# A matmul–GELU–matmul kernel: one store of the first result block moves from SyncE's DMA queue to GpSimd's

## The chip, the cores and the metric

The kernel runs on one core of one Trainium2 chip. The metric is the device time of one execution in microseconds (us), shown as the median of nine runs. A core has five engines with instruction streams of their own: TensorE (PE; its weight loads are a row of their own, PEld), VectorE (DVE), ScalarE (ACT), GpSimd (POOL) and SyncE (SP). They meet only through semaphores. SP computes nothing; here it issues DMAs and waits. A lower-case q after an engine's name (SPq) means its sequencer.

## The reference

```python
a: (1024, 1024), b: (1024, 2048), c: (2048, 1024), all float32, normal draws
h = np.matmul(a, b)
h = 0.5 * h * (1 + np.tanh(np.sqrt(2 / np.pi) * (h + 0.044715 * h ** 3)))
return np.matmul(h, c).astype(np.float32)
```

The result is 1024 x 1024 float32, 4 MiB, in rows of 128 (eight row tiles) by two halves of 512 columns.

## The kernel before

**Work.** `a` is loaded, cast to bf16 and transposed on PE; `b` and `c` are loaded and cast. The first product with GELU gives `h` transposed in bf16 (`hT`). Both products run in part or whole through the class `Seven`: a 2 x 2 block product in seven block products in place of eight, with sums and differences of blocks (`s1` to `s4` of the left factor, `t1` to `t4` of the right one) made on DVE in pieces of 128 x 1024. The object `two` is the second matrix product; `seven(two, done2, between2)` (L406) runs it. Its steps, in the order in which the program writes them: the block product P1, P2, P5, P6, P7, then the third and fourth ones. `between2` (L390) issues the DVE work between the steps: after P2 `two.s2(4)` and `two.s3(4)`, after P5 `two.t3(4)` and `two.s4(...)`, after P7 `two.t4`. All of it is one order written out by hand (`tc.manual_schedule()`), each engine runs its list in that order.

**Result tiles.** A finished 128 x 512 piece of the result is a tile `ot`, made by DVE: `plus` (L289, add of PSUM and a saved partial sum, at L291), or the copy at L386 in `done2`. These tiles turn in four buffers (tag "o"), so the fifth one must wait until the first one's store has landed. The first three come from P2 (blocks (0,0), j = 0, 1, 2: rows 0 to 383 of the left half), the fourth and fifth are the j = 0 and j = 1 tiles of P7. The last row tile of block (0,0) (j = 3) is done at the very end, in two pieces of 128 x 256 (L340 to L343).

**Stores.** `done2(i, l, j, p)` (L383) calls `store` (L380), which issues one DMA on the queue of the engine `eng`, or on SP's where none is given:

```python
def store(mt, q0, w, ot, eng=None):
    (eng or nc.sync).dma_start(out=out[ts(mt, 128), ds(q0, w)], in_=ot)
```

SP issues 8 loads (L68, L71) at the start and then all 17 stores: 15 of 256 KB (L381 from `done2`) and 2 of 128 KB (L381 from L343). POOL issues 20 loads (L93, L96, L99, L102), the last at 36.4 us, and nothing after them but the end of the program.

**Semaphores of the DMAs.** The framework gives every DMA of SP's queue one of eight semaphores in turn, DMAHW0 to DMAHW7, here called lanes, and every DMA of POOL's queue one of eight others, DMASW0 to DMASW7. A DMA adds 16 to its lane when all of it has landed. Before a DMA takes a lane again, its engine waits for the one that had it, eight DMAs earlier on the same queue. At the end of the program (the profile puts this at L432) SP waits for the final count of every lane, one instruction after the other, in this order:

```
1  DMASW7, DMASW6            6  DMAHW4, DMASW1
2  DMAHW0, DMASW5            7  DMAHW5, DMASW0
3  DMAHW1, DMASW4            8  DMAHW6, DVE
4  DMAHW2, DMASW3            9  DMAHW7, ACT
5  DMAHW3, DMASW2            then two drains, and a barrier of all engines
```

In the barrier each engine reports with a drain, POOL gathers the reports and releases all. SP's queue has 8 + 17 = 25 DMAs, numbers 0 to 24. The last store is number 24 and has lane DMAHW0, the one before it lane DMAHW7.

Of the kernel before, what the change touches and what calls it, by code (L numbers as in the profile page):

```python
# [19 lines left out]
def kernel(ctx, tc, a, b, c, out):  # L20
    nc = tc.nc
# [3 lines left out]
    H = 512  # L25
# [17 lines left out]
    def bank(i, shape=(128, H), dt=F32, name="ps"):  # L43
        return pp.tile(list(shape), dt, name=name, tag=f"bank{i}", padded_shape=None)

    def pieces(tag, bufs, shape, dt, name):
        return small.tile(shape, dt, name=name, tag=tag, bufs=bufs)
# [219 lines left out]
    p = bank(7)  # L267
# [4 lines left out]
    for n in range(8):  # L272
        h, t = divmod(n, 4)
        p = bank(n)
# [105 lines left out]
    def store(mt, q0, w, ot, eng=None):  # L380
        (eng or nc.sync).dma_start(out=out[ts(mt, 128), ds(q0, w)], in_=ot)  # L381

    def done2(i, l, j, p):  # L383
        if (i, l) == (1, 0):
            ot = pieces("o", 4, [128, H], F32, "ot")
            nc.vector.tensor_copy(ot, p)  # L386
            p = ot
        store(4 * i + j, l * H, H, p)

    def between2(n):  # L390
        if n == "P1":
# [11 lines left out]
        elif n == "P73":  # L403
            two.t4(two.t[1], 4)

    seven(two, done2, between2)  # L406


# [28 lines left out]
```

## Time and profile before

| | |
|---|---|
| median of 9 runs | 120.52 us (120.37 to 120.74) |
| the profiled execution | 120.40 us, of which the span of the profile is 118.6 us |
| granted TensorE clock | 0.996 |
| PE busy | 111.9 us (94% of the span) |
| DVE busy | 88.5 us (75%) |
| ACT busy | 52.7 us (44%) |
| POOL busy | 14.6 us (12%) |
| DMA, SP's queue (q1) | 5648 packets, 8.39 MB |
| DMA, POOL's queue (q0) | 5952 packets, 8.39 MB |
| HBM | 20.97 MB read, 4.19 MB written |

The span runs from the first instruction to the last; 1.8 us of the execution's time lie outside it. PE is busy nearly throughout, but that says nothing of the last microseconds: there the work is over and the program waits for its last store and closes. Times below are counted from the start of the span.

### The profile page before, as it was taken

Reading aid. Unit: us, or ns where it says so; the run is one execution under the profiler, and the core shown is the slowest. Engines: PE = TensorE matmul, PEld = TensorE weight load, DVE = VectorE, ACT = ScalarE, POOL = GpSimd, SP = SyncE. Lnnn points to the kernel's source line nnn. Section 1 sums busy time; section 2 is a strip of 40 time slices with the busy share of each in tenths; the row PEclk is TensorE's granted clock in tenths of the full one; section 3 lists DMA queues with packets and bytes.
Section 4 is the critical chain, followed back from the end, with each engine's and each line's share of the span. In section 5 each row is a group of like instructions: output and inputs, shape, how many; then the busy total and the mean of one; then the engine's idle time right before and its main releaser. Section 6 shows DMA issues by size and latency. Waiting matters only on the chain.

```text
span 118.6 us, 1473 instructions
## 1 busy us (share of the span) xinstructions
PE 111.9 (94%) x558; PEld 72.9 (61%) x558; DVE 88.5 (75%) x93; ACT 52.7 (44%) x86; POOL 14.6 (12%) x27
## 2 busy tenths in 40 slices
PE   6887999999999999999999999999999999999970
PEld 2544445654444446888886444588888888888850
DVE  0243689489058899796879999999999986944760
ACT  5046491006657789856589348700033982000000
POOL 2003976363222000000000000000000000000000
PEclk9999999999999999999999999999999999999998
DMA  3999999999999999994000000070000002024992
GB/s 91 293 371 369 338 202 211 198 205 205 208 210 210 211 210 211 211 211 88 3 3 0 6 0 0 0 265 0 0 0 0 6 4 84 0 93 176 361 351 81
DMA packets 11606, 16.86 MB, mean 142 GB/s; under 512 B 720, under 2 KB 6096, under 8 KB 11600
## 3 DMA queue, kind: packets, MB, share of 16 engines
q0 software_dynamic: 5952, 8.39, 39.8%
q1 hardware_dynamic: 5648, 8.39, 20.2%
q8 instruction: 4, 0.07, 0.2%
q14 instruction: 2, 0.02, 0.0%
HBM read 20.97 MB, written 4.19 MB: 212 GB/s over the span
## 4 chain that ended last, share of the span: by engine, by line
PE 86%; DMA 7%; SPq 2%; DVE 1%; issue 0%; DVEq 0%
PE ps L241 63%; PE ps L112 20%; DMA sta<-in_a_dram 7%; PE pt L187 2%; SPq L68 1%; SPq L71 1%; DVE ab L108 1%; PE pt L135 1%; DVE ot L342 0%; DVEq L108 0%
## 5 line engine op out<-in xcount | busy, mean ns | idle before, releaser
L112 PE MATMUL ps<-aT,b 128*128 128x512 bf16 x128 | 29.2, 379 | 1.4 <-DVE aT L136 0.8
L241 PE MATMUL ps<-x,s 128*128 128x512 f32 x128 | 29.5, 390 | 0.0
L241 PEld LDWEIGHTS ps<-x,s 128*128 128x128 f32 x128 | 24.0, 188 | 5.1 <-DVE ot L291 0.2
L112 PEld LDWEIGHTS <-b 128*128 128x128 bf16 x128 | 12.1, 97 | 15.2 <-issue 1.5
L241 PE MATMUL ps<-x,x 128*128 128x512 f32 x64 | 14.8, 389 | 0.0
L241 PE MATMUL ps<-c_sb,hT 128*128 128x512 bf16 (+1 forms) x72 | 14.2, 356 | 0.0
L241 PEld LDWEIGHTS ps<-x,x 128*128 128x128 f32 x64 | 12.0, 188 | 2.5
L286 ACT ACTIVATE v<-ps 128x512 f32<-128x512 f32 x8 | 4.8, 599 | 15.4 <-PE ps L241 15.4
L241 PE MATMUL ps<-x 128*128 128x512 f32 x48 | 11.2, 393 | 0.0
L241 PEld LDWEIGHTS <-hT 128*128 128x128 bf16 x72 | 6.9, 98 | 7.1 <-issue 0.5
L116 ACT ACTIVATE hT<-ps 128x512 bf16<-128x512 f32 x12 | 6.3, 603 | 11.0 <-PE ps L112 11.0
L241 PEld LDWEIGHTS ps<-x 128*128 128x128 f32 x48 | 9.0, 188 | 2.0
L276 DVE TENSOR_TENSOR half<-ps,half 128x512 f32<-128x512 f32 x8 | 5.5, 692 | 5.5 <-PE ps L112 5.1
L199 DVE TENSOR_TENSOR x<-c_sb 128x1024 fp32r<-128x1024 bf16 x8 | 9.2, 1219 | 0.0
L291 DVE TENSOR_TENSOR ot<-ps,v 128x512 f32<-128x512 f32 x8 | 5.3, 686 | 4.7 <-DMA out_dram<-ot 3.9
L291 DVE TENSOR_TENSOR ot<-ps,u 128x512 f32<-128x512 f32 x8 | 5.4, 690 | 2.9 <-ACT u L286 2.9
L141 ACT ACTIVATE b<-stb 128x512 bf16<-128x512 f32 (+1 forms) x9 | 4.7, 573 | 6.3 <-DMA stb<-in_b_dram 6.3
L116 ACT ACTIVATE hT<-ot 128x512 bf16<-128x512 f32 x12 | 6.9, 624 | 1.1 <-DVE ot L291 1.1
L241 PE MATMUL ps<-aT,b 128*128 128x512 bf16 x32 | 7.1, 379 | 0.0
L102 POOL DMA_DIRECT2D c_sb<-in_c_dram x8 | 5.7, 712 | 10.2 <-DMA b<-in_b_dram 10.2
L116 ACT ACTIVATE hT<-half 128x512 bf16<-128x512 f32 x8 | 5.0, 630 | 2.6 <-DVE half L276 2.6
L108 DVE CAST ab<-sta 128x1024 bf16<-128x1024 f32 x3 | 2.1, 695 | 5.1 <-DMA sta<-in_a_dram 5.1
(49 smaller groups left out, 116.4 us busy)
## 6 DMA issues: line engine op xcount, KB each, us to landing
c_sb<-in_c_dram POOLq DMA_DIRECT2D x8, 512.0 KB, 19.9
out_dram<-ot SPq DMA_DIRECT2D x15, 256.0 KB, 2.1
sta<-in_a_dram SPq DMA_DIRECT2D x4, 512.0 KB, 6.7
stb<-in_b_dram SPq DMA_DIRECT2D x4, 512.0 KB, 8.8
b<-in_b_dram POOLq DMA_DIRECT2D x4, 512.0 KB, 13.8
a<-in_a_dram POOLq DMA_DIRECT2D x4, 256.0 KB, 5.9
b<-in_b_dram POOLq DMA_DIRECT2D x4, 256.0 KB, 9.2
out_dram<-ot SPq DMA_DIRECT2D x2, 128.0 KB, 2.0
```

What stands on the lines that cost most here:

```text
L68: nc.sync.dma_start(out=sta[:, h, q], in_=av[:, 4 * h:4 * h + 4, ds(q * 256, 256)])
L102: nc.gpsimd.dma_start(out=c_sb[:, t:t + 2], in_=cv[:, t:t + 2])
L108: nc.vector.tensor_copy(dst, src)
L112: nc.tensor.matmul(p, b1[:, k, ts(t, 128)], aT[:, h, k], start=(k == k0), stop=(k == k1 - 1))
L116: nc.scalar.activation(hT[h][:, t], p, AF.Gelu_apprx_tanh)
L141: nc.scalar.activation(b1[:, k, ds(c * H + i * (H // n), H // n)], stb[:, c, k, r], AF.Copy)
L187: nc.tensor.transpose(pt[:, k, ts(n, 128)], a2[h, m][:, n, ts(k, 128)], ident)
L199: nc.vector.tensor_tensor(out=dst[:, r], in0=x[:, r], in1=y[:, r], op=op)
L241: nc.tensor.matmul(p[:, ds(c0, w)], l[:, k, ts(j, 128)], r[:, k, ds(c0, w)], start=(start and k == 0), stop=(k == self.kt - 1), skip_group ...
L276: nc.vector.tensor_tensor(out=half[:, h, t], in0=p, in1=half[:, h, t], op=ADD)
L286: nc.scalar.activation(st, p, AF.Copy)
L291: nc.vector.tensor_tensor(out=ot, in0=p, in1=st, op=ADD)
```

## The change

One argument of one call. `done2` passes POOL's queue for the tile with i + j + l = 0, which is the first store of all (block (0,0), j = 0), and nothing (so SP's queue) for the others:

```diff
             ot = pieces("o", 4, [128, H], F32, "ot")
             nc.vector.tensor_copy(ot, p)
             p = ot
-        store(4 * i + j, l * H, H, p)
+
+
+        store(4 * i + j, l * H, H, p, nc.gpsimd if i + j + l == 0 else None)
```

The tile, its 256 KB and its place in the result stay the same. Two lines are added, so what the profile of before calls L432 is L434 after. In the built program SP has 24 DMAs (8 loads, 16 stores) where it had 25, and one wait less; POOL has 21 DMAs where it had 20, and one wait more. The instructions of PE, DVE and ACT and their order are the same. Every later store of SP's queue has a lane one lower than before, so the waits of DVE for buffers of tag "o" name other lanes: the fifth tile waits for DMASW4 where it waited for DMAHW0. The closing waits stand in the same order as above. SP's last store is now number 23 and has lane DMAHW7, the one before it DMAHW6.

## The prediction

> **What bounds the kernel now.** I read the chain of waits first. From 39.66 us on it is PE alone, then one DVE add, and there the work ends:
>
> ```profile
> 39.66 75.22 PE ps L241 x344
> 114.89 0.02 issue
> 114.91 0.42 DVE ot L342
> ```
>
> Columns are start, length, what. The add ends at 114.91 + 0.42 = 115.33 us, but the span is 118.6 us. So 3.3 us belong to no engine's work, and they are where this change acts. Next I asked for the last store (first the issues from 114 to 115 us, then from 115 to 116 us):
>
> ```profile
> L381 SPq DMA_DIRECT2D out_dram<-ot x2: 332/352/371, 114.0 to 114.5; - x2
> DMA to landing us min/median/max: 2.1/2.1/2.1
> ...
> L381 SPq DMA_DIRECT2D out_dram<-ot x1: 332/332/332, 115.4 to 115.4; - x1
> DMA to landing us min/median/max: 1.9/1.9/1.9
> ```
>
> Durations are in ns, least/median/most. To the nanosecond, the records of the trace say: last store issued at 115.359, landed at 117.30; the one before it issued at 114.488, landed at 116.59. Then the instructions of the closing line, L432, first those from 115.7 to 117.3 us, then those from 117.35 to 118 us:
>
> ```profile
> L432 SPq EVENT_SEMAPHORE  x1: 28/28/28, 115.7 to 115.7; - x1
> ...
> L432 SPq EVENT_SEMAPHORE  x7: 27/28/28, 117.4 to 117.7; - x7
> L432 SPq DRAIN  x2: 7/7/7, 117.8 to 117.9; - x2
> ```
>
> An EVENT_SEMAPHORE here is one of SP's closing waits. One passes at 115.737 (the loads' lanes, long full). The next passes at 117.316, 16 ns after the last store's landing: it is the wait for DMAHW0, the lane of that store. Only then do the seven waits for DMAHW1 to DMAHW7 run, at 117.378, 117.442, 117.504, 117.563, 117.624, 117.684 and 117.745. All their stores had landed by 116.59, so none of the seven waits for anything; but each takes its turn, and the first drain follows at 117.810. POOL's gather passes at 117.901, 32 ns after SP's second drain starts (117.869): SP's report is the last. PE's closing drain had ended at 114.92 and DVE's at 115.38. So the end of the span hangs on SP's list of waits.
>
> **The change, part by part.** *The closing waits.* Seven waits that need nothing take 117.745 - 117.316 = 0.429 us, 61 ns each (28 ns executing, the rest between instructions). After the change the last store has lane DMAHW7, which stands last. The waits for DMAHW0 to DMAHW6 pass while the last store is under way: the latest of them is DMAHW6, the store of 116.59 us, and one step of 61 ns later SP stands at DMAHW7 at about 116.66, 0.64 us before 117.30. That is the cover which hides them. If it were gone, with the second to last store landing as late as the last, one step (0.06 us) would show, no more. So DMAHW7 passes at 117.316 and the drain at 117.381 rather than 117.810: minus 0.429 us. All behind it (drains, gather, release, clearing of semaphores, second barrier) keeps its lengths and moves up by that.
>
> *The store that leaves SP.* SP issued it at 76.508 for 0.360 us. SP then waits for DVE before each of its later stores, so this frees nothing that ends later: 0. The lanes shift by one, but each store still waits for the one eight places earlier; the pairs are the same as before, and the last store (issue 115.36) waits for one that landed at 111.66: 0.
>
> *The store on POOL.* POOL's row shows no store, so I bound it by its loads, in both issue and landing:
>
> ```profile
> L96 POOL DMA_DIRECT2D b<-in_b_dram x4: 583/590/594, 14.0 to 15.6; - x4
> DMA to landing us min/median/max: 8.3/9.2/10.3
> ...
> L102 POOL DMA_DIRECT2D c_sb<-in_c_dram x8: 696/713/716, 22.6 to 36.4; - x8
> DMA to landing us min/median/max: 15.9/19.9/20.1
> ```
>
> Issue: 0.58 to 0.83 us (the most is one of the loads at L93); I take 0.59, L96 being 128 rows of 2 KB as the store is. Nothing is queued behind it on POOL but the end. Landing: at best SP's 2.1 us, at worst the 20.1 us of a load that stood in a line of others. I take some 3 us (SP's 2.1 plus the longer issue), as POOL's queue has been empty since 56.30 us, when the last load landed. Who waits for it? DVE's fifth result tile (L291), which begins at 96.90. Even at 20.1 us the store lands at 76.5 + 20.1 = 96.6: 0 at both ends. POOL's closing drain ran from 36.38 for 20.78 us to 57.16, 0.86 us behind its last landing; now it ends between 79.5 and 97.5, some 20 us ahead of the gather: 0.
>
> *DVE beside POOL's issue.* While POOL issues, DVE makes the pieces of s2, s3, t3 and s4 without a gap:
>
> ```profile
> 77.59 4.62 DVE L199 TENSOR_TENSOR s<-s,hT 128x1024 fp32r<-128x1024 f32 x4
> 82.13 4.63 DVE L199 TENSOR_TENSOR s<-hT,hT 128x1024 fp32r<-128x1024 bf16 x4
> 86.67 4.63 DVE L199 TENSOR_TENSOR x<-c_sb 128x1024 fp32r<-128x1024 bf16 x4
> 91.22 4.63 DVE L199 TENSOR_TENSOR x<-hT,s 128x1024 fp32r<-128x1024 bf16 x4
> 96.29 1.29 DVE L291 TENSOR_TENSOR ot<-ps,u 128x512 f32<-128x512 f32 x2 [0.45 <-ACT u L286]
> ```
>
> A delay D of DVE would reach PE first at t3, the third row: its last piece is done at 91.30, and P7, whose first weight load is at 90.96 and which takes a new piece every 0.453 us, wants it at 92.32. So 1.02 us of D is hidden. Past P7 it dies out in DVE's own 0.45 us of idle and 1.2 us or more ahead of each later use. Is there a delay at all? Two rows of the same DVE operation, the first with two of POOL's issues within it (25.02 and 26.24), the second with none:
>
> ```profile
> L199 DVE TENSOR_TENSOR x<-aT 128x2048 fp32r<-128x2048 bf16 x1 | 2.3, 2292 | 0.0
> L199 DVE TENSOR_TENSOR x<-b 128x2048 fp32r<-128x2048 bf16 x1 | 2.3, 2283 | 0.0
> ```
>
> D is 0.009 us by these, at most one whole issue of 0.83 us; both lie under 1.02: 0. POOL's issue was 0.713 us within the first row and 0.713 us beside no such operation, so it isn't held either.
>
> A rule speaks against the move. The Trainium skill, SBUF — State Buffer, section "A bandwidth-pool intuition that's wrong (but worth ruling out)", says that GpSimd cannot write its descriptors while DVE holds their shared port, and that a GpSimd DMA of 620 ns alone took 3100 ns beside a DVE copy; its section "Who interferes with whom" sees no such hold for adds and subtractions of two tensors, which are what runs here. The rows side with the second; by the first the store would land about 2.5 us later (an estimate from that page), long ahead of 96.90, and the sum would be the same.
>
> **The sum.** The profiled execution: 120.40 - 0.429 = 119.97 us, its span 118.6 - 0.43 = 118.2 us. It lies 0.12 us under the median of the runs shown, so for the median 120.52 - 0.43 = 120.09 us.
>
> **The rivals.** *No change.* Something else closes the program: another engine's report comes after SP's, or the waits cost the same in front of the landing as behind it. For it: the gain is 0.36% of the time and sits in records of 28 ns. Against: PE's and DVE's reports are in by 115.38, 2 us early, POOL's drain 20 us early, and SP stands idle from 115.74 to 117.32. It would also be so if the closing waits were placed in another order, but in the built program they stand as before. It decides if the gather comes no sooner than 117.90: 120.52 us.
>
> *Slower: POOL's store holds DVE up.* Place: the s2 pieces at 77.59, by a store under way until it lands rather than for its issue alone. Price: D - 1.02 on PE, less 0.43; it decides from D = 1.45 us on. With D as long as a landing of the loads at L93 (5.9 us, median) it is 5.9 - 1.02 - 0.43 = +4.45, 124.97 us. For it: DVE has no idle time from 77.59 to 95.84. Against: the 2292 ns beside 2283, where loads were landing throughout the first.
>
> **How the numbers follow.** Forecast 0.83, no change 0.11, slower 0.06. The prediction is the forecast's 120.09. Its own range is the scatter of the runs about their median, -0.15 and +0.22: 119.94 to 120.31. The range of 8 in 10 goes a little past both ends, towards the no-change case: 119.90 to 120.50. A measurement of this kernel tells 0.2%, 0.24 us, from no change. The forecast's gain exceeds that by 0.19 us, so of its 0.83 I give 0.02 to "within": faster 0.81, same 0.13, slower 0.06.
>
> **What would show it.** Right: in the changed profile one closing wait of SP's passes at the last landing, and the drains follow it directly, with seven waits before that time rather than behind it; the span is 118.2 us; PE's chain from 39.66 still lasts 75.2 us; L199's pieces still take 1.22 us. Wrong: waits still in a row behind the landing, a gap on PE at about 91 us, L199 above 1.3 us between 76 and 82 us, DVE waiting at 96.9 for the store, or POOL's drain next to the gather.

## The result, and the profile after

| | before | changed |
|---|---|---|
| median | 120.60 us (31 runs, 120.37 to 120.76) | 120.14 us (10 runs, 119.95 to 120.44) |
| profiled execution | 120.40 us, span 118.6 us | 119.99 us, span 118.2 us |
| ratio of the times | | 0.9964, 95% interval 0.9955 to 0.9972 |

The changed kernel is 0.36% faster, 0.43 us. First the chain of waits of the changed kernel (start, length, what), its last lines:

```profile
39.66 75.22 PE ps L241 x344
114.88 0.02 issue
114.91 0.42 DVE ot L342
```

These are the lines of before, within a hundredth: from 39.66 us on the work runs and ends at the same times in the two profiled executions. That is luck, as the experiments show, but it leaves the last three microseconds alone to be compared. The last store of the changed kernel (issues from 115 to 117 us), then the instructions of the closing line, now L434: those from 115.7 to 116.7 us, and the first two rows of those from 117.2 to 118 us:

```profile
L381 SPq DMA_DIRECT2D out_dram<-ot x1: 332/332/332, 115.4 to 115.4; - x1
DMA to landing us min/median/max: 2.0/2.0/2.0
...
L434 SPq EVENT_SEMAPHORE  x8: 27/28/28, 115.7 to 116.6; - x8
...
L434 SPq DRAIN  x3: 7/7/7, 117.4 to 117.7; - x3
L434 SPq EVENT_SEMAPHORE  x2: 17/22/28, 117.3 to 117.6; - x2
```

Of SP's nine closing waits eight have now passed by 116.6 us, where before one had. One is left for the landing: the first of the two in the last row, at 117.334 in the records (the other one, of 17 ns at 117.6, belongs to the barrier). The drains follow from 117.399 on. SP's own waits show the same from another side, first before, then in the changed kernel:

```profile
SPq L432 <- DMA out_dram<-ot: 1.5, 1, 1.5
...
SPq L434 <- DMA out_dram<-ot: 1.1, 2, 0.7
```

Columns are the wait's total, how often, the longest. SP now stops twice, 1.1 us in all, for the last two landings (116.60 and 117.32 us); before it stopped once for 1.5 us, for the last landing, with the rest of its list still to do.

### The profile page after: what moved, and what is told of

Its sections match the earlier page's. It is cut to its first block, busy times and chain, and to the rows that moved or that the text cites. A ratio compares the mean times of both kernels' runs of the same rounds, so it can differ in the third digit from the quotient of the medians.

```text
span 118.2 us, 1473 instructions
## 1 busy us (share of the span) xinstructions
PE 111.5 (94%) x558; PEld 72.7 (61%) x558; DVE 88.5 (75%) x93; ACT 52.7 (45%) x86; POOL 15.2 (13%) x28
## 3 DMA queue, kind: packets, MB, share of 16 engines
q0 software_dynamic: 6032, 8.65, 40.3%
q1 hardware_dynamic: 5504, 8.13, 19.9%
## 4 chain that ended last, share of the span: by engine, by line
PE 90%; DMA 4%; DVE 2%; SPq 0%; ACT 0%; issue 0%
PE ps L241 64%; PE ps L112 23%; DMA stb<-in_b_dram 4%; PE pt L187 2%; PE pt L135 1%; DVE aT L136 1%; SPq L68 0%; ACT b L141 0%; DVE ot L342 0%
## 5 line engine op out<-in xcount | busy, mean ns | idle before, releaser
L241 PE MATMUL ps<-x,s 128*128 128x512 f32 x128 | 29.5, 390 | 0.0
L241 PEld LDWEIGHTS ps<-x,s 128*128 128x128 f32 x128 | 24.0, 188 | 5.1 <-DVE ot L291 0.2
L241 PE MATMUL ps<-x,x 128*128 128x512 f32 x64 | 14.8, 389 | 0.0
L241 PE MATMUL ps<-c_sb,hT 128*128 128x512 bf16 (+1 forms) x72 | 14.2, 356 | 0.0
L241 PEld LDWEIGHTS ps<-x,x 128*128 128x128 f32 x64 | 12.0, 188 | 2.5
L241 PE MATMUL ps<-x 128*128 128x512 f32 x48 | 11.2, 393 | 0.0
L241 PEld LDWEIGHTS <-hT 128*128 128x128 bf16 x72 | 6.9, 98 | 7.0 <-issue 0.5
L241 PEld LDWEIGHTS ps<-x 128*128 128x128 f32 x48 | 9.0, 188 | 2.0
L199 DVE TENSOR_TENSOR x<-c_sb 128x1024 fp32r<-128x1024 bf16 x8 | 9.2, 1218 | 0.0
L241 PE MATMUL ps<-aT,b 128*128 128x512 bf16 x32 | 7.1, 379 | 0.0
```

Source lines behind the costliest of these rows:

```text
L199: nc.vector.tensor_tensor(out=dst[:, r], in0=x[:, r], in1=y[:, r], op=op)
L241: nc.tensor.matmul(p[:, ds(c0, w)], l[:, k, ts(j, 128)], r[:, k, ds(c0, w)], start=(start and k == 0), stop=(k == self.kt - 1), skip_group ...
```

## The experiments

All of them are timed in five rounds beside the kernel before. A time of 0.4 us is small against a span that can start late, so for each profile I also give a time that does not depend on that: from the end of PE's last matmul (modelled by the profiler, the same way in every run) to the start of the last closing wait.

| run | DMAs in the eight lanes, lane of the last store | last landing, us | closing waits behind it that wait for nothing | last wait less PE's end, us | ratio to before (95%) |
|---|---|---|---|---|---|
| before | 25, DMAHW0 | 117.30 | 7 | 2.87 | 1 |
| changed | 24, DMAHW7 | 117.32 | 0 | 2.46 | 0.9964 (0.9955 to 0.9972) |
| e1_pool_and_25 | 25, DMAHW0 | 117.56 | 7 | 2.89 | 1.0003 (0.9994 to 1.0012) |
| e2_sp_32 | 32, DMAHW7 | 117.46 | 0 | 2.36 | 0.9955 (0.9942 to 0.9967) |
| e3_sp_29 | 29, DMAHW4 | 117.36 | 3 | 2.54 | 0.9979 (0.9960 to 0.9998) |
| e4_pool3_24 | 24, DMAHW7 | 117.40 | 0 | 2.46 | 0.9960 (0.9947 to 0.9972) |
| e5_last_two_queues | 24, DMAHW7 | 117.55 | 0 | 2.39 | 0.9958 (0.9943 to 0.9973) |
| e6_384_128 | 24, DMAHW7 | 117.28 | 0 | 2.42 | 0.9954 (0.9938 to 0.9971) |
| e7_384_128_act | 24, DMAHW6 (ACT) | 117.44 | 1 | 2.49 | 0.9968 (0.9955 to 0.9981) |
| e8_changed_again | 24, DMAHW7 | 117.71 | 0 | 2.47 | 0.9969 (0.9956 to 0.9982) |

The first four kernels use `store` with a table of cuts, so that an early store can be issued in several pieces and the count of SP's DMAs be set at will; the data stored is the same.

**The store on POOL, but 25 DMAs on SP again.**

```diff
+    CUT = {(1, 0): (256, 256)}
+
     def store(mt, q0, w, ot, eng=None):
-        (eng or nc.sync).dma_start(out=out[ts(mt, 128), ds(q0, w)], in_=ot)
+        at = 0
+        for n in CUT.get((mt, q0), (w,)):
+            (eng or nc.sync).dma_start(out=out[ts(mt, 128), ds(q0 + at, n)], in_=ot[:, at:at + n])
+            at += n
```

> The first store stays on POOL as in the changed kernel, and the second one is issued in two halves of 256 columns, so that SP's queue has 25 DMAs again and its last store has lane DMAHW0. Theory (the gain is the seven closing waits that pass before the last landing rather than behind it, 61 ns each): seven waits stand behind the last landing again, 0.43 us of them, and the time is that of before: ratio 1.000 (0.9985 to 1.0015). Rival A (the gain comes from the store having left SP's queue): ratio 0.9964, as the changed kernel had.

Measured: 1.0003 (0.9994 to 1.0012). Its closing instructions from 117.59 to 118.1 us:

```profile
L439 SPq EVENT_SEMAPHORE  x8: 28/28/28, 117.6 to 118.0; - x8
L439 SPq DRAIN  x1: 7/7/7, 118.1 to 118.1; - x1
```

Eight waits stand at and behind the landing of 117.56 again, the last at 118.004, and the whole gain is gone, although the first store is on POOL as in the changed kernel. So the move itself brings nothing that shows (the interval leaves 0.07 us faster to 0.14 us slower); what brings the gain is the number of DMAs that it leaves on SP.

**Nothing on POOL, 32 DMAs on SP.** The kernel before with `CUT = {(0, 0): (128,)*4, (1, 0): (128,)*4, (2, 0): (256, 256)}`.

> Nothing on POOL. The three stores of step P2 are issued on SP in 4, 4 and 2 pieces, so that SP's queue has 32 DMAs and its last store has lane DMAHW7. Theory: no closing wait behind the last landing but its own; 0.43 us less than before, ratio 0.9964 (0.995 to 0.998), although SP issues seven DMAs more. Rival A (the store must leave SP's queue): ratio 1.000 or above. If POOL's store cost DVE or PE something in the changed kernel (rival B), this run is faster than the changed kernel by that much.

Measured: 0.9955 (0.9942 to 0.9967). From 115.9 to 116.85 us its closing line reads

```profile
L437 SPq EVENT_SEMAPHORE  x8: 27/28/28, 116.0 to 116.8; - x8
```

which is the picture of the changed kernel. SP issues seven DMAs more than before and the kernel is faster all the same; rival A falls. Its interval overlaps the changed kernel's, so the runs do not tell the two apart, and show no cost of POOL's store. The 2.36 us in the table, where the changed kernel has 2.46, come from the last landing: it followed its issue by 1.85 us, against 1.94 to 1.96 in before, the changed kernel and the runs with the same last store of 128 KB, this one and the next excepted. The last packet ended 1.35 to 1.36 us behind the issue in all of them, so it is the landing's signal that came some 0.1 us sooner; why, no run shows.

**The dose: 29 DMAs on SP.** The kernel before with `CUT = {(0, 0): (128,)*4, (1, 0): (256, 256)}`.

> As the run before, but with 4 and 2 pieces for two stores: 29 DMAs on SP, last lane DMAHW4, so three waits (DMAHW5 to DMAHW7) stand behind the last landing where there were seven. Theory: 4 of 7 steps gained, 4 x 0.061 = 0.245 us, ratio 0.998 (0.9968 to 0.9992), and the profile shows 3 waits behind the landing. Rival A: 1.000.

Measured: 0.9979 (0.9960 to 0.9998). Its closing instructions from 117.35 to 117.42 us, and then the first row of those from 117.42 to 117.7 us:

```profile
L437 SPq EVENT_SEMAPHORE  x1: 28/28/28, 117.4 to 117.4; - x1
...
L437 SPq EVENT_SEMAPHORE  x3: 28/28/28, 117.4 to 117.6; - x3
```

The wait for the last landing passes at 117.378, the three behind it at 117.439, 117.499 and 117.560: 61 ns a step. Against before 4 x 0.061 = 0.245 us should be gone; 0.0021 of 120.61 us is 0.25 us, in an interval of 0.02 to 0.48 us. The profile settles the count and the step; the timing alone would only say that something is gained. From PE's end to the last wait the run is 0.34 us shorter than before (2.54 against 2.87): 0.245 us are the four steps, and 0.09 us the last landing, which here too came 1.85 us after its issue.

**Three stores on POOL.** The changed kernel with

```diff
-        store(4 * i + j, l * H, H, p, nc.gpsimd if i + j + l == 0 else None)
+        store(4 * i + j, l * H, H, p, nc.gpsimd if i + l == 0 and j < 3 else None)
```

and `CUT = {(4, 512): (256, 128, 128)}`.

> All three stores of step P2 are on POOL; one later store (the left tile of P7, j = 0, right lower block) is issued in three pieces, so that SP's queue has 24 DMAs and the last store lane DMAHW7, as in the changed kernel. Theory: POOL's stores cost nothing on the path of PE; ratio 0.9964 (0.995 to 0.998), L199 pieces still 1.22 us. Rival B (POOL's issues hold DVE): three times the hold; with one issue of 0.58 us held each, D = 1.74 us, 0.72 us more than the 1.02 us that P7 hides: ratio 1.002 and a gap on PE near 91 us.

Measured: 0.9960 (0.9947 to 0.9972). POOL's issues from 76 to 82 us, and DVE in time order beside and after them:

```profile
L385 POOL DMA_DIRECT2D out_dram<-ot x3: 540/565/582, 76.9 to 78.1; - x3
DMA to landing us min/median/max: 2.4/2.6/2.7
...
77.68 4.62 DVE L199 TENSOR_TENSOR s<-s,hT 128x1024 fp32r<-128x1024 f32 x4
82.22 4.62 DVE L199 TENSOR_TENSOR s<-hT,hT 128x1024 fp32r<-128x1024 bf16 x4
86.76 4.62 DVE L199 TENSOR_TENSOR x<-c_sb 128x1024 fp32r<-128x1024 bf16 x4
91.30 4.62 DVE L199 TENSOR_TENSOR x<-hT,s 128x1024 fp32r<-128x1024 bf16 x4
96.37 1.29 DVE L291 TENSOR_TENSOR ot<-ps,u 128x512 f32<-128x512 f32 x2 [0.46 <-ACT u L286]
```

The groups of four pieces take 4.62 us (4.62 to 4.63 before), beside three of POOL's issues; DVE keeps its idle time ahead of 96.37. Rival B falls.

**Two tries to go further, and a third.** With the closing waits hidden, what is left at the end is PE's end, the last add, one issue and one landing. The first try cuts the last 256 columns into two pieces on two queues (the edit in part):

```diff
-                ot = pieces("e", 2, [128, 256], F32, "ot")
-                nc.vector.tensor_tensor(out=ot, in0=p[:, r], in1=p1[3][:, r], op=ADD)
-                store(3, i * 256, 256, ot)
+                for c0, n, eng in ((0, 256, None),) if i == 0 else ((256, 128, nc.scalar), (384, 128, None)):
+                    r = ds(c0, n)
+                    ot = pieces(f"e{c0}", 1, [128, n], F32, "ot")
+                    nc.vector.tensor_tensor(out=ot, in0=p[:, r], in1=p1[3][:, r], op=ADD)
+                    store(3, c0, n, ot, eng)
```

> Tries to beat the changed kernel. The last 128 x 256 piece is added and stored in two pieces of 128 columns, the first stored on ACT's queue, the second on SP's; two stores of P2 are on POOL, so that SP's and ACT's queues together have 24 DMAs and the last store has lane DMAHW7. Theory: after the closing waits are hidden, the end hangs on PE's end, the last add, the issue (0.33 us) and the landing (2.0 us) of the last store alone; two adds of 128 columns end about 0.04 us later than one of 256, and a landing of 64 KB in place of 128 KB saves some 0.1 to 0.2 us if it depends on the size: ratio to before 0.9955 to 0.997. If the landing does not depend on the size: 0.9967.

Measured: 0.9958 (0.9943 to 0.9973), not to be told from the changed kernel. The store of 64 KB on SP landed 1.82 us after its issue, where the one of 128 KB took 1.96 us; the second add ended at 115.70, 0.53 us after PE, where the one add of the changed kernel ends 0.46 us after it. The last wait passes 2.39 us behind PE's end, in place of 2.46.

The second try cuts the last row tile into 384 and 128 columns, with both of its stores on SP (the edit in part; product, tile and store take the same `c0` and `n`):

```diff
-            for i in range(2):
-                r = ds(i * 256, 256)
+            for i, (c0, n) in enumerate(((0, 384), (384, 128))):
+                r = ds(c0, n)
```

> The changed kernel with its last row tile cut into 384 and 128 columns in place of 256 and 256. PE: the 8 matmuls of 384 columns take some 0.16 us each, the 8 of 128 no less than their weight loads, 0.098 us each: PE ends about 0.3 us later; the last add is some 0.13 us shorter and the last store is 64 KB. Theory: the end moves with PE's end, the add and the landing and nothing else; 0.0 to 0.2 us slower than the changed kernel, ratio to before 0.9965 to 0.998.

Measured: 0.9954 (0.9938 to 0.9971). The expectation for PE was wrong: the 16 matmuls of this tile take 1.92 us as before, and PE ends at 114.882 against 114.871. The add was shorter as expected, but now SP was in the way, as its issues from 115 to 115.2 us and from 115.4 to 115.6 us show:

```profile
L381 SPq DMA_DIRECT2D out_dram<-ot x1: 332/332/332, 115.1 to 115.1; - x1
...
L381 SPq EVENT_SEMAPHORE  x1: 17/17/17, 115.4 to 115.4; - x1
L381 SPq DMA_DIRECT2D out_dram<-ot x1: 383/383/383, 115.5 to 115.5; - x1
DMA to landing us min/median/max: 1.8/1.8/1.8
```

The last add had ended at 115.228, its store was issued at 115.483: SP was still issuing the store of 384 columns until 115.391, and then had to pass the wait for the next lane, which was long full (the 17 ns row). So the third try gives that store to ACT's queue (`store(3, c0, n, ot, nc.scalar if i else None)`), and the changed kernel ran beside it.

> The run with 384 and 128 columns, but the last store (64 KB) goes to ACT's queue. There the last add had ended at 115.23 us, and SP could issue its store only at 115.48, as it was still issuing the store of 384 columns. Theory (the end hangs on the last landing alone): issue on ACT at about 115.26, landing 1.8 us later at 117.06; the store of 384 columns lands at about 117.01; the last of the closing waits passes near 117.08 where the changed kernel's passes at 117.33: 0.25 us less than the changed kernel, ratio to before 0.994 to 0.995. If ACT's store lands no earlier than SP's did: 0.996 as the changed kernel.

> The changed kernel itself beside the run before, on the same chip. Theory: 0.9964 (0.995 to 0.9975).

Measured: 0.9968 (0.9955 to 0.9981) and 0.9969 (0.9956 to 0.9982): no gain. The issue did come earlier, 0.03 us behind the add. But the landing did not (issues from 115 to 116 us):

```profile
L381 SPq DMA_DIRECT2D out_dram<-ot x1: 332/332/332, 115.2 to 115.2; - x1
L381 ACTq DMA_DIRECT2D out_dram<-ot x1: 374/374/374, 115.4 to 115.4; - x1
...
DMA to landing us min/median/max: 2.0/2.0/2.0
```

64 KB on ACT's queue took 2.03 us, issued 0.20 us behind a store of 192 KB that landed 0.25 us ahead of it. The packets show where the time went: those of the 64 KB began 1.16 us behind the issue, while the packets of the 192 KB were moving from 116.04 to 116.74 us; in the first try the store on ACT's queue had its first packet 0.88 us behind the issue. That the two stores share the DMA engines would explain it; it was not tried apart. In this kernel the framework gave the store on ACT lane DMAHW6, so one step of 62 ns stands behind its landing again. No version beats the changed kernel beyond its interval.

## Why the prediction was right, point by point

**Closing waits, the term that sets the sum.** Predicted: minus 0.429 us, seven steps of 61 ns. Measured between the two profiles: the last closing wait passes at 117.334 in place of 117.745, minus 0.411 us. The missing 0.018 us is the last landing, 117.32 in place of 117.30. The profiled execution took 119.99 us, predicted 119.97; the median 120.14, predicted 120.09. That it is the steps, and not the store's leaving SP, is shown by the runs with 25, 29 and 32 DMAs: 7, 3 and 0 steps behind the last landing, whatever queue the first store has. In the last two the last landing was some 0.1 us shorter besides, which is no part of the prediction and stays open. The median was forecast from 120.52 us, the nine runs then shown; from the 120.60 of all 31 the same sum gives 120.17.

**The cover.** Predicted: SP reaches DMAHW7 at about 116.66, 0.64 us early. It passed DMAHW6 at 116.616, one step later stood at DMAHW7 at about 116.68, and waited there 0.64 us for the landing at 117.32. The price if that cover is gone (one step) was not tried by itself; with ACT's store in DMAHW6 landing last, one step of 62 ns stood behind it.

**The store that leaves SP.** Predicted: nothing. The next store of SP was issued at 77.106 us in both kernels. The reason given is not quite right: not each of SP's later stores waits for DVE. Those at 105.569, 108.542 and 109.509 us of before come right behind another issue; but the store that leaves stands far ahead of them.

**The store on POOL.** Predicted: issue 0.59 us, landing some 3 us, nothing behind it. This is the row of the changed kernel that before did not have (issues from 76.7 to 77.05 us):

```profile
L381 POOL DMA_DIRECT2D out_dram<-ot x1: 580/580/580, 76.8 to 76.8; - x1
...
DMA to landing us min/median/max: 2.6/2.6/2.6
```

The issue was of the size of L96, the row that I took. It landed at 79.40, 17.5 us before DVE wants the buffer at 96.90, so the bound of 20.1 us was far from being needed. The "some 3 us" were a little too many: 2.1 plus the longer issue (0.59 less 0.36) is 2.3, and the landing took 2.62. One thing was not foreseen: the two stores that SP issued behind it landed 2.70 and 2.81 us after their issue, where they took 2.17 and 2.24 before. Their buffers are wanted again only after 97 us. POOL's closing drain ended at 80.31, 0.91 us behind that landing (predicted: 79.5 to 97.5).

**DVE beside it.** Predicted D between 0.009 and 0.83 us, all of it hidden. Measured: none. The changed kernel's groups from 77 to 97 us (total, mean ns, idle before):

```profile
L199 DVE TENSOR_TENSOR s<-hT,hT 128x1024 fp32r<-128x1024 bf16 x4 | 4.6, 1216 | 0.0
L199 DVE TENSOR_TENSOR s<-s,hT 128x1024 fp32r<-128x1024 f32 x4 | 4.6, 1216 | 0.0
```

Before, the same pieces took 1218 to 1220 ns. So the caution of the Trainium skill (SBUF — State Buffer, "A bandwidth-pool intuition that's wrong (but worth ruling out)"), a GpSimd DMA held beside DVE, did not show for these two-tensor adds and subtractions: POOL's issue took 0.58 us among them, the store landed in 2.6 us. That is the side of its section "Who interferes with whom". No run here has a DVE copy in its place.

**The rivals.** No change: SP's report was indeed the last one; nothing else came between. Slower by DVE: D was nothing, where 1.45 us would have been needed.

**The range.** 119.90 to 120.50 held 120.14. The scatter that I took from the runs is, as far as the profiles show, mostly one of the start, see below: the changed kernel's profiled execution lies 0.15 us under its median, before's lies 0.20 us under the median of its 31 runs.

## What to carry to other kernels

Read the profile past the end of the work: between the last add and the end of the span lay 3.3 us here, and 0.43 us of them were a list of waits of which only the first one waited. Where a framework deals out completion semaphores in turn and closes by waiting for each in a fixed order, the last transfer should hold the one that is waited for last; the count of DMAs on that queue decides it, and any store cut in two, or moved, turns it. So an edit that adds or removes one DMA on that queue can move such a kernel's time by up to seven steps of 61 ns either way (here from 25 to 24 and back), which has nothing to do with the transfer that was edited.

## What the runs showed of the hardware that was not expected

- The start of a profiled execution varies by as much as this change is worth. PE's L241 part begins at 39.66 us in both profiles compared above, at 39.73 to 39.87 in the first four experiments, and at 40.05 in the changed kernel run again, whose second load landed at 6.88 us where it was 6.46; the part itself takes 75.22 to 75.26 us in these seven profiles. Against an absolute time, 0.4 us of a tail would be lost in that.
- POOL takes up a store later than SP. The first tile's add ends at 76.48 us in both kernels; SP issued its store at 76.508, 0.03 us later, POOL at 76.780, 0.30 us later.
- The same 256 KB were 144 packets on SP's queue (5648 became 5504) and 80 on POOL's (5952 became 6032).
- A landing hardly depends on the size at the end of this kernel: 1.85 to 1.96 us for 128 KB, 1.80 us for 64 KB issued 0.42 us or more behind the store before it, 1.82 us for 64 KB issued 0.19 us behind another 64 KB, 2.03 us for 64 KB issued 0.20 us behind 192 KB.
